# Gate and up projections of an FFN as seven products of quarters

## The chip, the cores and the metric

The kernel runs on one core of one Trainium2 chip. The metric is the device time of one execution in microseconds (us). Five engines work beside each other, each through its own instructions in order: PE (matmul; PEld is its weight load), DVE (vector), ACT (scalar), POOL (GpSimd) and SP (here it only issues DMAs). Matmuls read SBUF and write PSUM; DMAs move data between HBM and SBUF.

## The reference

Two layers of a decoder trunk on 512 tokens of width 1024. Each layer is a half-weight SwiGLU FFN, a token mixer (sparse attention and retention), cross-attention into 256 memory tokens, and a second half-weight FFN; each of them has an RMSNorm before and after it. All is float32. The FFN, which the change is about:

```python
def rms_norm(x, g):
    y = x * lax.rsqrt(jnp.mean(x * x, axis=-1, keepdims=True) + EPS)
    return y * g
def swiglu(x, w_gate, w_up, w_down):          # 1024 -> 2816 -> 1024
    return (jax.nn.silu(x @ w_gate) * (x @ w_up)) @ w_down
y = swiglu(rms_norm(x, ffn1_pre_g[l]), ffn1_w_gate[l], ffn1_w_up[l], ffn1_w_down[l])
x = x + 0.5 * rms_norm(y, ffn1_post_g[l])
```

## The kernel before, in words

Activations lie transposed: 8 tiles `x[c]` of 128 features by 512 tokens. A product of float32 precision is made of three matmuls on numbers split into a high and a low part (`mm3`, L113 to L116: high x high, high x low, low x high). The splits cost an ACT copy (the high part) and a DVE subtraction (the low part): for weights in `unit` (L85, L86), for activations in `split` (L122, L123) and `split_x` (L183, L184).

An FFN has 22 blocks of 128 hidden features, in three groups of 8, 7 and 7. For a block, `ffn` loads two weight units of 128 x 1024 (gate and up, 512 KB each, `nc.sync.dma_start`, three load buffers `raw`, four split buffers `whi` and `wlo`), and runs 2 x 8 chunks x 3 matmuls of 512 columns into two PSUM tiles `ps_gu`. L274 to L280 multiply by the inverse norm `bc`, form the SwiGLU with a tanh, and split the result into `hh` and `hl`. After a group comes its down projection: 8 output chunks `ps_dn`, each with 3 matmuls per block, added into `y[c]` (L299 copies in the first group, L301 adds later). In the last group the squares of `y[c]` are summed (`sumsq`, L153 on ACT and L154 on POOL, the last one on DVE), then `postnorm` takes the inverse norm through PE transposes and a Newton iteration on DVE, adds to `x[c]` and splits it for the next stage.

The last FFN of the program ends in `down_halves`: the last group of 7 blocks is done for the first 256 tokens, then for the others, and the norm and the output of the first half lie beside the matmuls of the second. `filler` and `prep` are pieces of cross-attention's keys, values and memory splits, put between stages.

The instructions are written per engine in the order that a scheduler of the framework draws up when the kernel is built: by program order, by what is ready, and by free buffers, with durations that it assumes. At run time every engine keeps that order. Load buffers are freed by the split's DVE part; the SP queue issues a load as soon as its buffer is free.

Of the kernel before, what the change touches and what calls it, by code (L numbers as in the profile page):

```python
# [9 lines left out]
F32 = mybir.dt.float32  # L10
# [7 lines left out]
P = 128  # L18
T = 512
# [6 lines left out]
GROUPS = ((0, 8), (8, 15), (15, 22))  # L26
# [21 lines left out]
def trunk(ctx: ExitStack, tc: tile.TileContext, a: dict, out: bass.AP):  # L48
# [9 lines left out]
    slots = {"b": 24, "xs": 16, "h": 16, "kv": 6}  # L58
# [20 lines left out]
    def unit(src, n):  # L79

        raw = wp.tile([P, 1024], F32, name="raw", tag="raw", bufs=3)[:, :n]
        nc.sync.dma_start(raw, src)
        hi = wp.tile([P, 1024], F32R, name="whi", tag="whi", bufs=4)[:, :n]
# [5 lines left out]
    def raw_unit(src, n):  # L89
        raw = wp.tile([P, 1024], F32, name="raw", tag="raw", bufs=3)[:, :n]  # L90
        nc.sync.dma_start(raw, src)
        return raw
# [4 lines left out]
    first = {0: unit(a["ffn1_gu"][0, 0, 0], 1024)}  # L97
    for c in range(1, 4):
        nc.sync.dma_start(x[c], a["xT"][c])
    first[1] = unit(a["ffn1_gu"][0, 0, 1], 1024)  # L100
# [12 lines left out]
    def mm3(ps, ah, al, bh, bl, start, stop):  # L113
        pe.matmul(ps, ah, bh, start=start, stop=False)  # L114
        pe.matmul(ps, ah, bl, start=False, stop=False)  # L115
        pe.matmul(ps, al, bh, start=False, stop=stop)  # L116
# [40 lines left out]
    def rms_cols(ssq, n, width):  # L157
# [6 lines left out]
        dve.tensor_reduce(t, ps[:, :width].rearrange("p (j n) -> p j n", n=P), axis=AX.X, op=ALU.add)  # L164
        v = tiny("rms_v", nt)
        dve.tensor_scalar(v, t, 1.0 / n, EPS, op0=ALU.mult, op1=ALU.add)
        return newton(v, nt)
# [17 lines left out]

    def gcols(l, col):
        return small[l][:, col : col + NC]

    def prenorm():

        xh, xl = [h for h, _ in xs], [lo for _, lo in xs]
        xs.clear()
        ssq, part = None, None
# [9 lines left out]
        return xh, xl, cols, bc  # L203

    def postnorm(y, ssq, gains, nxt, ts_=slice(0, T)):

        w = ts_.stop - ts_.start
        ps = row_bc(rms_cols(ssq[:, ts_], D, w), w // P)
        for c in range(NC):
# [3 lines left out]
            split_x(c, nxt, ts_)  # L213
# [43 lines left out]
    def ffn(l, which, gains, nxt, filler=None, prep=None, halves=False):  # L257
        gu, dn = FF_UNITS[which]
        if filler:
            filler()  # L260
        xh, xl, cols, bc = prenorm()
        y, ssq = [None] * NC, None
        for gi, (f0, f1) in enumerate(GROUPS):
            hh, hl = [], []
            for f in range(f0, f1):
                w = [first.pop(b) if b in first else unit(a[gu][l, f, b], 1024) for b in range(2)]
                pss = [acc("ps_gu") for _ in range(2)]
                for ts_ in HALVES if halves and f == 0 else (slice(0, T),):
                    for (wh, wl), ps in zip(w, pss):
                        for k in range(NC):  # L270
                            s = slice(k * P, (k + 1) * P)
                            mm3(ps[:, ts_], wh[:, s], wl[:, s], xh[k][:, ts_], xl[k][:, ts_], k == 0, k == NC - 1)
                g1 = big("g1")
                dve.tensor_tensor(g1, pss[0], bc, op=ALU.mult)  # L274
                th = big("th")
                act.activation(th, g1, AF.Tanh, scale=0.5)
                u1 = big("u1")
                dve.tensor_tensor(u1, pss[1], bc, op=ALU.mult)  # L278
                dve.scalar_tensor_tensor(g1, th, 1.0, g1, op0=ALU.add, op1=ALU.mult)
                dve.scalar_tensor_tensor(u1, g1, 0.5, u1, op0=ALU.mult, op1=ALU.mult)  # L280
                h_, l_ = split(u1, "h", tag="h")
                hh.append(h_)
                hl.append(l_)
            n = f1 - f0
            last = gi == len(GROUPS) - 1
            if prep and last:
                prep()
            if last and nxt is None:
                down_halves(a[dn][l], f0, n, hh, hl, y, gains)
                return  # L290
            for c in range(NC):
                wh, wl = unit(a[dn][l, c][:, f0 * P : f1 * P], n * P)
                ps = acc("ps_dn")
                for k in range(n):
                    s = slice(k * P, (k + 1) * P)
                    mm3(ps, wh[:, s], wl[:, s], hh[k], hl[k], k == 0, k == n - 1)
                if gi == 0:
# [4 lines left out]
                if last:  # L302
                    ssq = sumsq(ssq, y[c], c, dve if c == NC - 1 else pool)
        postnorm(y, ssq, gains, nxt)

    def down_halves(src, f0, n, hh, hl, y, gains):

        w = []
        for c in range(NC):
            if c < 4:  # L310
                wh, wl = unit(src[c][:, f0 * P : (f0 + n) * P], n * P)
                w.append([(wh[:, k * P : (k + 1) * P], wl[:, k * P : (k + 1) * P]) for k in range(n)])
            else:
                raw = raw_unit(src[c][:, f0 * P : (f0 + n) * P], n * P)
                parts = []
                for k0 in (0, 4):
                    m = min(4, n - k0) * P
                    h_, l_ = big("dh", F32R, tag="xs")[:, :m], big("dl", F32R, tag="xs")[:, :m]
# [624 lines left out]
```

## Time and profile before

| | |
|---|---|
| time of the kernel, median of 3 | 2508.59 us (2506.43 to 2508.6) |
| time of the profiled execution | 2508.29 us |
| its span, first to last instruction | 2506.5 us |
| busy: PE, PEld, DVE, ACT, POOL | 2431.5, 2020.5, 1400.2, 902.4, 258.8 us |
| mean granted TensorE clock | 0.995 |
| DMA | 233.62 MB, mean 93 GB/s |

Matmuls overlap in the pipeline, so the duration of one (389 ns) is longer than its distance from the next; what a matmul costs is read from the distance. Idle time of an engine is put down to the instruction that ended it. A line of the profile (L114) is a line of the kernel printed above, and can be that of a helper which many stages call.

### The profile page before, as it was taken

How to read it: one execution, taken by the hardware profiler on the slowest of the kernel's cores; microseconds unless marked ns; L12 is line 12 of the kernel's file. 1: busy time of each engine (PE TensorE's matmuls, PEld its weight loads, DVE VectorE, ACT ScalarE, POOL GpSimd, SP SyncE). 2: the span in 40 equal slices, each digit the busy share in tenths (PEclk: the TensorE clock that was granted, in tenths of full speed). 3: DMA queues.
4: the chain of work that ended last, by engine and by line, in shares of the span. 5: the costliest groups of instructions: out<-in, count | busy, mean ns of one | idle time of the engine just before them, and what ended most of it. 6: DMA issues, size and time to landing. Idle time of an engine off the chain costs nothing. (4 is left out here: it accounts for less than half of the span.)

```text
span 2506.5 us, 30782 instructions
## 1 busy us (share of the span) xinstructions
PE 2431.5 (97%) x12052; PEld 2020.5 (81%) x12052; DVE 1400.2 (56%) x2536; ACT 902.4 (36%) x1480; POOL 258.8 (10%) x218
## 2 busy tenths in 40 slices
PE   8999999999999999999999999999999998999997
PEld 6888878888877878888878888868888777888887
DVE  6434458465776484344484344584657766634454
ACT  4322243255344443222343222332553443322222
POOL 0000022001040120000120000130010402100002
PEclk9999999999999999999999999999999999999999
DMA  4333333411232233233333333324112222232321
GB/s 173 98 100 94 99 121 108 143 45 34 76 109 84 93 101 93 101 93 100 110 98 96 101 93 101 106 89 150 44 35 70 93 76 68 86 100 92 102 90 62
DMA packets 74593, 233.62 MB, mean 93 GB/s; under 512 B 8272, under 2 KB 17744, under 8 KB 74448
## 3 DMA queue, kind: packets, MB, share of 16 engines
q1 hardware_dynamic: 65232, 222.21, 27.9%
q10 hardware_dynamic: 9216, 9.44, 1.2%
q8 instruction: 95, 1.56, 0.3%
q14 instruction: 50, 0.41, 0.1%
HBM read 229.53 MB, written 2.10 MB: 92 GB/s over the span
## 5 line engine op out<-in xcount | busy, mean ns | idle before, releaser
L85 ACT ACTIVATE whi<-raw 128x1024 fp32r<-128x1024 f32 (+2 forms) x402 | 417.8, 1041 | 1097.6 <-PE ps_gu L115 324.0
L86 DVE TENSOR_TENSOR wlo<-raw,whi 128x1024 fp32r<-128x1024 f32 (+2 forms) x402 | 491.2, 1223 | 292.7 <-ACT whi L85 284.4
L114 PE MATMUL ps_gu<-xsh,whi 128*128 128x512 f32 (+1 forms) x1424 | 552.3, 389 | 13.8 <-ACT whi L85 9.3
L115 PE MATMUL ps_gu<-xsl,whi 128*128 128x512 f32 (+1 forms) x1424 | 555.0, 390 | 9.9 <-DVE xsl L184 9.7
L116 PE MATMUL ps_gu<-xsh,wlo 128*128 128x512 f32 (+1 forms) x1424 | 552.8, 388 | 0.0
L115 PEld LDWEIGHTS ps_gu<-xsl,whi 128*128 128x128 f32 x1424 | 268.6, 189 | 71.2 <-DVE xsl L184 17.7
L114 PEld LDWEIGHTS ps_gu<-xsh,whi 128*128 128x128 f32 x1424 | 269.0, 189 | 69.2 <-ACT whi L85 9.2
L116 PEld LDWEIGHTS ps_gu<-xsh,wlo 128*128 128x128 f32 x1424 | 268.8, 189 | 55.4 <-DVE wlo L86 1.8
L154 POOL TENSOR_TENSOR ssq<-ssq,sq 128x512 f32<-128x512 f32 (+1 forms) x84 | 131.4, 1564 | 1708.7 <-ACT sq L153 1705.6
L115 PE MATMUL ps_dn<-hl,whi 128*128 128x512 f32 (+1 forms) x704 | 268.5, 382 | 2.4 <-DVE hl L123 2.4
L114 PE MATMUL ps_dn<-hh,whi 128*128 128x512 f32 (+1 forms) x704 | 268.2, 381 | 0.0
L116 PE MATMUL ps_dn<-hh,wlo 128*128 128x512 f32 (+1 forms) x704 | 268.0, 381 | 0.0
L278 DVE TENSOR_TENSOR u<-ps_gu,rstd_bc 128x512 f32<-128x512 f32 x88 | 60.8, 691 | 215.4 <-PE ps_gu L116 215.3
L274 DVE TENSOR_TENSOR g<-ps_gu,rstd_bc 128x512 f32<-128x512 f32 x88 | 60.8, 691 | 183.9 <-PE ps_gu L116 179.4
L115 PEld LDWEIGHTS ps_dn<-hl,whi 128*128 128x128 f32 x704 | 132.3, 188 | 28.9 <-DVE hl L123 3.8
L114 PEld LDWEIGHTS ps_dn<-hh,whi 128*128 128x128 f32 x704 | 132.4, 188 | 26.2 <-ACT hh L122 0.5
L116 PEld LDWEIGHTS ps_dn<-hh,wlo 128*128 128x128 f32 x704 | 132.4, 188 | 25.1
L301 DVE TENSOR_TENSOR y<-ps_dn,y 128x512 f32<-128x512 f32 x56 | 38.7, 691 | 132.3 <-PE ps_dn L116 132.3
L115 PE MATMUL ps_fm<-xsl,whi 128*128 128x512 f32 x256 | 103.2, 404 | 4.0 <-DVE xsl L184 3.8
L114 PE MATMUL ps_fm<-xsh,whi 128*128 128x512 f32 x256 | 103.0, 404 | 0.0
L116 PE MATMUL ps_fm<-xsh,wlo 128*128 128x512 f32 x256 | 101.3, 396 | 0.6 <-DVE wlo L86 0.6
L612 ACT ACTIVATE p<-p,smx 128x512 f32<-128x512 f32 (+3 forms) x128 | 70.5, 552 | 87.2 <-DVE smx L610 87.0
(226 smaller groups left out, 3723.0 us busy)
## 6 DMA issues: line engine op xcount, KB each, us to landing
raw<-in_ffn_gu_dram SPq DMA_DIRECT2D x176, 512.0 KB, 3.3
raw<-in_ffn_dn_dram SPq DMA_DIRECT2D x64, 448.0 KB, 3.3
raw<-in_ffn_dn_dram SPq DMA_DIRECT2D x32, 512.0 KB, 3.5
raw<-in_win_fm_dram SPq DMA_DIRECT2D x32, 512.0 KB, 3.3
raw<-in_wk_dram SPq DMA_DIRECT2D x16, 512.0 KB, 3.5
raw<-in_cmp_w_dram SPq DMA_DIRECT2D x16, 512.0 KB, 3.7
raw<-in_wout_dram SPq DMA_DIRECT2D x16, 512.0 KB, 3.5
raw<-in_wv_dram SPq DMA_DIRECT2D x16, 512.0 KB, 3.5
```

Of the source, the lines that this page charges most:

```text
L85: act.activation(hi, raw, AF.Copy)
L86: dve.tensor_tensor(lo, raw, hi.bitcast(F32), op=ALU.subtract)
L114: pe.matmul(ps, ah, bh, start=start, stop=False)
L115: pe.matmul(ps, ah, bl, start=False, stop=False)
L116: pe.matmul(ps, al, bh, start=False, stop=stop)
L154: eng.tensor_tensor(acc_t, acc_t, sq, op=ALU.add)
L274: dve.tensor_tensor(g1, pss[0], bc, op=ALU.mult)
L278: dve.tensor_tensor(u1, pss[1], bc, op=ALU.mult)
L301: dve.tensor_tensor(y[c], ps, y[c], op=ALU.add)
L612: act.activation(pr[i], pr[i], AF.Exp, bias=m, scale=-1.0, accum_out=sums[:, i : i + 1])
```

## The change

Two blocks make a pair; an FFN has 11 pairs. The weights of gate and up for a pair lie in HBM as four quarters q0 to q3 of 128 x 1024 (first block with input chunks 0 to 3, the same with chunks 4 to 7, second block likewise; each with gate and up side by side). The operands are x in quarters as well: chunks 0 to 3 or 4 to 7, first or second half of the tokens.

The first two pairs of an FFN are computed as before from quarters (`plain`). The other nine use seven products instead of eight (the Winograd form of Strassen's scheme): seven weight operands (four quarters and sums of them) by seven operands of x (pieces and sums of them, made once per FFN in `combos`), each 2 x 4 x 3 matmuls of 256 columns. Sums of products are made partly in PSUM (a product added to what an earlier one left) and partly by DVE and POOL. The weight sums are made by DMAs of POOL's queue which add a quarter from HBM to a tile in SBUF (`accum_op`). Weight splits go from 4 to 7 per pair. The signs are folded into the operands, and the inverse norm before the up product is left out and put into the norm after the FFN (`cols` in `rms_cols`).

The down projection works on groups of 4 blocks, and of 2 in the end; the group of two pairs is projected after the products of the pair that follows. Load buffers go from 3 to 6, work slots (tag "b") from 24 to 18, "xs" from 16 to 24, "h" from 16 to 8; the mixer's queries and keys move into load buffers, and some tiles change their tag. The first pair's operands and weights, and the filler, are asked for ahead of the norm of the stage before (`ffn_first`).

```diff
-    slots = {"b": 24, "xs": 16, "h": 16, "kv": 6}
+    slots = {"b": 18, "xs": 24, "h": 8, "kv": 6, "onsa": 1}
...
+    def split_s(c, g, ts_=slice(0, T)):
+        k = c % 4
+        for u, half in enumerate(HALVES):
...
+            if c < 4:
+                if k % 2 == 0:
+                    ops["t", u] = big("x1h", F32R, tag="xs"), big("x1l", F32R, tag="xs")
+                ops[u + 1, k] = hi, lo = [t[:, HALVES[k % 2]] for t in ops["t", u]]
+                act.activation(hi, x[c][:, half], AF.Copy, scale=g[:, c : c + 1])
+                dve.scalar_tensor_tensor(lo, x[c][:, half], g[:, c : c + 1], hi.bitcast(F32), op0=ALU.mult, op1=ALU.subtract)
...
+    def combos(g):
...
+        for k in range(4):
+            b = []
+            for c in (k, k + 4):
+                xg = big("xg")
+                act.activation(xg, x[c], AF.Copy, scale=g[:, c : c + 1])
+                b += [xg[:, HALVES[0]], xg[:, HALVES[1]]]
+            t5, t7 = big("xt"), big("xt")
+            dve.tensor_tensor(t5[:, :256], b[1], b[0], op=ALU.subtract)
+            pool.tensor_tensor(t7[:, :256], b[3], b[1], op=ALU.subtract)
+            dve.tensor_tensor(t5[:, 256:], b[3], t5[:, :256], op=ALU.subtract)
+            pool.tensor_tensor(t7[:, 256:], t5[:, 256:], b[2], op=ALU.subtract)
...
+    class Pair:
...
+        def add(self, t, q):
+            pool.dma_start(t, self.quarter(q), accum_op=ALU.add)
+            return t
+        def raw(self, n):
+            if n == 1:
+                self.t = self.load(0)
+                return self.t
+            if n == 7:
+                return self.add(self.t, 2)
+            if n == 5:
+                self.u = self.load(2)
+                return self.add(self.u, 3)
+            if n == 6:
+                return self.add(self.u, 0)
+            if n == 3:
+                return self.add(self.u, 1)
+            return self.load({2: 1, 4: 3}[n])
...
+        def product(self, n, ps, o, start=True):
+            if n not in self.w:
+                self.weights(n)
+            wh, wl = self.w.pop(n)
+            for u in range(2):
+                for k in range(4):
+                    s = slice(u * 512 + k * P, u * 512 + (k + 1) * P)
+                    xh, xl = ops[o, k]
+                    mm3(ps[:, HALVES[u]], wh[:, s], wl[:, s], xh, xl, start and u == 0 and k == 0, u == 1 and k == 3, not start)
...
+        def p1(self):
+            self.A = acc("ps_gu")
+            self.product(1, self.A, 1)
+            self.s1 = self.kept(self.A)
+        def p2(self):
+            self.product(2, self.A, 3, start=False)
+        def p7(self):
+            self.C = aux("ps_gc")
+            self.product(7, self.C, 7)
+            self.s7 = self.kept(self.C)
+        def p5(self):
+            self.B = acc("ps_gu")
+            self.product(5, self.B, 5)
+            self.s5 = self.kept(self.B)
+        def p6(self):
+            self.product(6, self.B, 6, start=False)
+            self.e = big("ge")
+            dve.tensor_tensor(self.e, self.B, self.s1, op=ALU.subtract)
+            pool.tensor_tensor(self.s5, self.e, self.s5, op=ALU.subtract)
+        def p4(self):
+            self.product(4, self.C, 8, start=False)
+            dve.tensor_tensor(self.s7, self.e, self.s7, op=ALU.subtract)
+            dve.tensor_tensor(self.s5, self.s5, self.C, op=ALU.subtract)
+        def p3(self):
+            ps = acc("ps_gu")
+            self.product(3, ps, 4)
+            dve.tensor_tensor(self.e, ps, self.e, op=ALU.subtract)
+        def swiglu(self, bc, hs, tag="h"):
+            for q in ((self.A, self.e), (self.s5, self.s7)):
+                g1, th = big("g1"), big("th")
+                for ts_, t in zip(HALVES, q):
+                    dve.tensor_tensor(g1[:, ts_], t[:, :256], bc[:, ts_], op=ALU.mult)
+                act.activation(th, g1, AF.Tanh, scale=0.5)
+                dve.scalar_tensor_tensor(g1, th, 1.0, g1, op0=ALU.add, op1=ALU.mult)
+                for ts_, t in zip(HALVES, q):
+                    dve.tensor_tensor(g1[:, ts_], g1[:, ts_], t[:, 256:], op=ALU.mult)
+                hs.append(split(g1, "h", 0.5, tag=tag))
...
+        ORDER = "p1", "p5", "p2", "p7", "p6", "p4", "p3"
...
+        for p in pairs[:2]:
+            for f in range(2):
+                p.plain(f, bc, hs)
+                if p is pairs[0] and f == 1:
+                    combos(gcols(l, G_F1PRE if which == "ffn1" else G_F2PRE))
+        f0 = 0
+        for p in pairs[2:]:
+            final = p is pairs[-1]
+            for n in ORDER:
+                getattr(p, n)()
+            if len(hs) == 4:
+                down(f0, hs, False)
+                f0, hs = f0 + 4, []
+            p.swiglu(bc, hs, "xs" if final else "h")
...
+        down(f0, hs, True)
+        postnorm(y, state["ssq"], gains, nxt, cols=(cols, sq))
```

## Rows read from the trace of the kernel before

**Rows 1.** The page, parts 1 and 2: busy time and share; granted clock by fortieths.

```profile
PE 2431.5 (97%) x12052; PEld 2020.5 (81%) x12052; DVE 1400.2 (56%) x2536; ACT 902.4 (36%) x1480; POOL 258.8 (10%) x218
PEclk9999999999999999999999999999999999999999
```

**Rows 2.** Windows: us, busy (x instructions) of each engine, PEclk, DMA share, GB/s.

```profile
145.00:221.00 76.00, 76.00 (x337) 62.90 (x337) 37.27 (x46) 22.59 (x28) 0.00 (x0) 1.00 0.30 92
221.00:259.00 38.00, 38.00 (x169) 31.47 (x168) 15.96 (x18) 8.60 (x9) 0.00 (x0) 1.00 0.33 103
755.00:839.00 84.00, 83.96 (x414) 66.44 (x413) 57.72 (x115) 43.69 (x88) 0.00 (x0) 0.99 0.28 88
2108.00:2152.00 44.00, 35.30 (x209) 30.43 (x208) 35.93 (x90) 19.06 (x34) 15.69 (x17) 0.92 0.19 61
```

**Rows 3.** Timeline of PE: start, us, instruction; a run of 48 matmuls of 512 columns.

```profile
864.70 0.39 PE L114 MATMUL ps_o<-xoh,whi 128*128 128x512 f32 x1
...
875.35 0.39 PE L116 MATMUL ps_o<-xoh,wlo 128*128 128x512 f32 x1
875.58 0.28 PE L114 MATMUL ps_mk<-memg,whi 128*128 128x256 f32 x1
```

**Rows 4.** Timeline of PE in the last down projection: matmuls of 256 columns, 21 apart.

```profile
2489.35 0.28 PE L114 MATMUL ps_dn<-hh,dh 128*128 128x256 f32 x1
...
2491.87 0.28 PE L114 MATMUL ps_dn<-hh,dh 128*128 128x256 f32 x1
```

**Rows 5.** Groups by form, DVE and ACT: xcount | busy us, mean ns | idle before.

```profile
L86 DVE TENSOR_TENSOR wlo<-raw,whi 128x1024 fp32r<-128x1024 f32 x336 | 420.0, 1251 | 276.1 <-ACT whi L85 273.7 <-PE ps_o L116 1.8
L274 DVE TENSOR_TENSOR g<-ps_gu,rstd_bc 128x512 f32<-128x512 f32 x88 | 60.8, 691 | 183.9 <-PE ps_gu L116 179.4 <-ACT rstd_bc L202 4.4
L301 DVE TENSOR_TENSOR y<-ps_dn,y 128x512 f32<-128x512 f32 x56 | 38.7, 691 | 132.3 <-PE ps_dn L116 132.3
L329 DVE TENSOR_TENSOR y<-ps_dn,y 128x256 f32<-128x256 f32 x16 | 6.7, 422 | 18.9 <-PE ps_dn L116 18.7
L85 ACT ACTIVATE whi<-raw 128x1024 fp32r<-128x1024 f32 x336 | 355.6, 1060 | 909.5 <-issue 301.8 <-PE ps_gu L115 235.1 <-PE ps_dn L115 168.8
L122 ACT ACTIVATE hh<-u 128x512 fp32r<-128x512 f32 x88 | 55.7, 633 | 63.2 <-DVE u L280 63.1
```

**Rows 6.** Groups by form, POOL; the largest two.

```profile
L154 POOL TENSOR_TENSOR ssq<-ssq,sq 128x512 f32<-128x512 f32 x65 | 116.6, 1794 | 1054.2 <-ACT sq L153 1051.5 <-issue 1.2
L154 POOL TENSOR_TENSOR ssq<-ssq,sq 128x256 f32<-128x256 f32 x19 | 14.8, 777 | 654.4 <-ACT sq L153 654.1
```

**Rows 7.** The page, parts 3 and 6: the main DMA queue; issues with landing time.

```profile
q1 hardware_dynamic: 65232, 222.21, 27.9%
...
raw<-in_ffn_gu_dram SPq DMA_DIRECT2D x176, 512.0 KB, 3.3
```

**Rows 8.** Waits of the SP queue: us in total, times, longest.

```profile
SPq L82 <- DVE wlo L86: 2035.9, 361, 37.4
```

**Rows 9.** Timeline of DVE, 899 to 907 us; POOL adds until 904.15.

```profile
899.34 1.98 DVE L86 TENSOR_TENSOR wlo<-raw,whi 128x1024 fp32r<-128x1024 f32 x1
...
905.89 1.21 DVE L86 TENSOR_TENSOR wlo<-raw,whi 128x1024 fp32r<-128x1024 f32 x1
```

**Rows 10.** Timeline of POOL over the same stretch.

```profile
898.49 5.66 POOL L154 TENSOR_TENSOR ssq<-ssq,sq 128x512 f32<-128x512 f32 x3
```

**Rows 11.** Timeline of DVE in the tail: halves' evictions, norm and last adds.

```profile
2471.25 0.42 DVE L329 TENSOR_TENSOR y<-ps_dn,y 128x256 f32<-128x256 f32 x1 [2.10 <-PE ps_dn L116]
...
2481.20 0.74 DVE L329 TENSOR_TENSOR y<-ps_dn,y 128x256 f32<-128x256 f32 x2
...
2493.40 0.43 DVE L154 TENSOR_TENSOR ssq<-ssq,sq 128x256 f32<-128x256 f32 x1 [0.55 <-ACT sq L153]
```

**Rows 12.** Timeline of all engines at the end of the second FFN.

```profile
1253.71 1.74 POOL L154 TENSOR_TENSOR ssq<-ssq,sq 128x512 f32<-128x512 f32 x1 [3.02 <-ACT sq L153]
...
1258.98 0.68 DVE L154 TENSOR_TENSOR ssq<-ssq,sq 128x512 f32<-128x512 f32 x1
```

More of the change, by code (lines that the diff above doesn't have):

```diff
@@ L111, in trunk, with mm3 @@
             lst.append(hg)
[L113 to L116, printed above, removed]
+    def mm3(ps, ah, al, bh, bl, start, stop, more=False):
+        pe.matmul(ps, ah, bh, start=start, stop=False, skip_group_check=more)
+        pe.matmul(ps, ah, bl, start=False, stop=False, skip_group_check=more)
+        pe.matmul(ps, al, bh, start=False, stop=stop, skip_group_check=more)
     def split(src, name, gain=None, tag="b"):
@@ L202, in prenorm, with postnorm @@
         act.activation(bc, ps, AF.Copy)
-        return xh, xl, cols, bc
-    def postnorm(y, ssq, gains, nxt, ts_=slice(0, T)):
+        return cols, bc
+    def postnorm(y, ssq, gains, nxt, ts_=slice(0, T), cols=None):
         w = ts_.stop - ts_.start
-        ps = row_bc(rms_cols(ssq[:, ts_], D, w), w // P)
+        if ts_.start == 0 and nxt[0]:
+            nxt[0]()
+        ps = row_bc(rms_cols(ssq[:, ts_], D, w, cols), w // P)
         for c in range(NC):
@@ L212, in postnorm @@
             (dve if c == 0 else pool).tensor_tensor(x[c][:, ts_], x[c][:, ts_], t, op=ALU.add)
-            split_x(c, nxt, ts_)
+            (split_s if nxt[0] else split_x)(c, nxt[1], ts_)
     def out_proj(src, l, oh, ol):
@@ L286, in ffn, with ffn_first, run @@
[L286 to L292, printed above, removed]
+                for ts_, t in zip(HALVES, q):
+                    dve.tensor_tensor(g1[:, ts_], g1[:, ts_], t[:, 256:], op=ALU.mult)
+                hs.append(split(g1, "h", 0.5, tag=tag))
+    warm = {}
+    def ffn_first(l, which, filler=None):
+        def run():
+            if filler:
+                filler()
+            ps_ = warm[l, which] = [Pair(a[FF_UNITS[which][0]][l], j) for j in range(NPAIR)]
+            for q in range(2):
+                ps_[0].w["q", q] = split_unit(ps_[0].load(q))
+        return run
@@ new lines, in ffn, with weights, down @@
+    def ffn(l, which, gains, nxt, prep=None):
+        dn = FF_UNITS[which][1]
+        pairs = warm.pop((l, which))
+        y, state = [None] * NC, {"ssq": None}
+        ORDER = "p1", "p5", "p2", "p7", "p6", "p4", "p3"
+        def weights(f0, n):
+            per = 1024 // (n * P)
+            for c0 in range(0, NC, per):
+                raw = wp.tile([P, 1024], F32, name="raw", tag="raw", bufs=6)
+                nc.sync.dma_start(raw.rearrange("p (c n) -> p c n", c=per),
+                                  a[dn][l, c0 : c0 + per, :, f0 * P : (f0 + n) * P].rearrange("c p n -> p c n"))
+                wh, wl = split_unit(raw)
+                for u in range(per):
+                    yield c0 + u, [(wh[:, s], wl[:, s]) for s in
+                                   (slice((u * n + k) * P, (u * n + k + 1) * P) for k in range(n))]
+        def down(f0, hs, final):
+            n = len(hs)
+            for c, w in weights(f0, n):
@@ L301, in ffn @@
                     dve.tensor_tensor(y[c], ps, y[c], op=ALU.add)
[L302 to L318, printed above, removed]
-                    act.activation(h_, raw[:, k0 * P : k0 * P + m], AF.Copy)
-                    dve.tensor_tensor(l_, raw[:, k0 * P : k0 * P + m], h_.bitcast(F32), op=ALU.subtract)
-                    parts += [(h_[:, k * P : (k + 1) * P], l_[:, k * P : (k + 1) * P]) for k in range(m // P)]
-                w.append(parts)
-        for ts_ in HALVES:
+                if final:
+                    state["ssq"] = sumsq(state["ssq"], y[c], c, dve if c == NC - 1 else pool)
@@ L687, in to_fm @@
                 pe.transpose(pt[:, i * P : (i + 1) * P], tiles[i], ident)
-            h_, l_ = split(pt, "o", sm[:, G_NSA + c : G_NSA + c + 1], tag="h")
+            h_, l_ = split(pt, "o", sm[:, G_NSA + c : G_NSA + c + 1], tag="xs" if c < 4 else "h")
             oh.append(h_)
@@ L818, in xattn @@
                     mm3(ps, v_h[:, fs], v_l[:, fs], pTh[m], pTl[m], m == 0, m == 1)
-                h_, l_ = split(ps, "xo", tag="h")
+                h_, l_ = split(ps, "xo", tag="xs" if f < 4 else "h")
                 oh.append(h_)
```

170 lines of the change are left out of this document (108 added, 62 removed).

## The prediction

> **What bounds the kernel now.** I read the page's first two parts, then windows over stages, then a timeline of single matmuls. PE is busy 97% of the span, at full granted clock (2.4 GHz) in all forty slices [rows 1]. Inside an FFN there is nothing else: in 76 us of gate and up projections PE is busy for all 76 us, DVE for 37, ACT for 23; in the 38 us of down projection after it PE again fills the stretch [rows 2]. So a microsecond less of matmuls there is a microsecond less of time, as long as DVE, ACT and the DMAs can follow. Where PE is not full is the border between stages: in the 44 us at the entry of the last FFN it is busy 35 [rows 2].
>
> The price of a matmul is its distance from the next. With 512 columns 48 of them take 875.58 - 864.70 = 10.88 us, 226.7 ns each [rows 3]. With 256 columns 21 take 2491.87 - 2489.35 = 2.52 us, 120.0 ns each [rows 4]. Two halves thus cost 240.0 where a whole costs 226.7: each matmul has 13.3 ns that don't shrink with its columns.
>
> **The change, part by part.** The sum is made against the profiled execution, 2508.3 us (span 2506.5 and 1.8 around it), 0.3 under the median of 2508.59.
>
> *Seven products.* A pair of blocks had 2 blocks x 2 (gate, up) x 8 chunks x 3 = 96 matmuls of 512 columns: 21.76 us. It gets 7 products x 2 x 4 x 3 = 168 of 256 columns: 20.16 us. The arithmetic falls by 1/8, but the 13.3 ns come 72 times more often, so the gain is 1.60 us a pair, and 57.6 us for 9 pairs x 4 FFNs. The Trainium skill (TensorE: Matmul & The Clock Gate, Back-to-back issue gap) gives columns / 2.4 + 2.5 ns for a warm matmul. By that, an estimate, the pair would go from 20.7 to 18.3 us, the 36 pairs would give 85 us, and the time would come out at 2460 us. This trace disagrees at both widths (226.7 and 120.0 ns for 215.8 and 109.2), so it gets no chance of its own.
>
> *Plain pairs.* The other 2 pairs read quarters: per block 48 matmuls of 256 and 24 of 512, 5.76 + 5.44 = 11.20 us against 48 of 512, 10.88. For 16 blocks +5.1, less 0.6 for the one that already ran in halves: +4.5 us.
>
> *Down projection.* 22 blocks x 8 x 3 matmuls stay, in groups of 4,4,4,4,4,2 for 8,7,7. On PE that is free. In the last FFN only 2 blocks instead of 7 are done in token halves, which takes cover away from the tail. Now the first half's last eviction is at 2471.25, DVE then does that half's norm until 2481.20, PE goes on with 20.16 us of second-half matmuls meanwhile, and the last square sum is at 2493.40, 13.1 us before the end [rows 11]. After, the second half has 5.76 us of matmuls, done before DVE comes back; its evictions (8 x 0.42 [rows 5]) and POOL's chain of square sums (6 x 0.78 [rows 6]) follow in a row, so that I put the last square sum some 16 us behind the first half's end instead of 22.2. Counted with PE: before 20.16 + 35.3 to the end, after 27.2 (five blocks whole) + 5.8 + 29.1 = 62.1 us, so +7 us.
>
> *End of the other three FFNs.* With 2 blocks in the last group PE makes an output chunk in 6 x 0.2267 = 1.36 us, but its square sum takes POOL 1.79 [rows 6]. Six of those are a chain of 10.7 us that starts about 4 us into the 10.9 us group, and with the last add ends some 4.5 us behind PE. Now a chunk has 21 x 0.2267 = 4.76 us, the sums come 5.27 us apart, POOL is done long before the last one [rows 12], and that is one eviction, one square and one add behind PE: 0.69 + 0.63 + 0.68 = 2.0 us. +2.5 us each, +7; at nothing where memory keys or values fill PE meanwhile.
>
> *Entry.* Operands come in half-token pieces, with gate and up of the first block together. Three entries stay paced by the same chain; I take 0, from -5 to +5 each. The last loses something: chunks 4 to 7 of the first block need both token halves. +4 us, of 0 to 8; PE is idle 8.7 of the 44 us there already [rows 2].
>
> *Buffers elsewhere.* The work slots go from 24 to 18; the mixer gives six back by moving queries and keys to the load buffers. Cross-attention doesn't, and PE is full there now [rows 2], so a stall is seen: +3 us over both layers, of 0 to 10.
>
> *DVE and ACT in a product pair.* DVE: 7 weight splits x 1.25, 4 differences x 0.69, and for two blocks 2 x (4 half products x 0.42 + 2 x 0.69) [rows 5]: 8.75 + 2.76 + 6.12 = 17.6 us. The down projection adds per pair 2 splits and 4 evictions, 5.3 us: 22.9 of PE's 20.16 + 10.88 = 31.0 us. ACT: 9 splits x 1.06 and some 7 passes x 0.63 = 14 us. Both fit on average. Down projection comes behind every second pair only, so in the pair without it DVE has 17.6 of 20.2 us. I take 0.3 us of stall a pair, +11 us; the ends are 0 and, were DVE's 17.6 to grow by a third, 23.5 for 20.2 in 16 such pairs, +53.
>
> *Weight sums by DMA.* No accumulating DMA is in this trace, nor any issued by POOL. Nearest is a plain load of the same 512 KB: 3.3 us to landing [rows 7]. The queue moved 222.21 MB in 27.9% of 2506.5 us [rows 7], 318 GB/s while busy, so 1.65 us of the 3.3 are transfer. An accumulation can't land sooner than the load it contains (lower end 3.3); it must also read what it adds to, 5.0 with one more transfer; 10 is three loads one behind the other (upper end). I take 6 us with POOL's issue. What it may cost follows from the order 1,5,2,7,6,4,3: one tile carries q2 (+q3) for product 5, +q0 for 6, +q1 for 3, each addition waiting for the split before it. With four split buffers, the split of 5 can start when the product four places ahead of it ends, 5.8 us before product 1; product 3 starts 17.3 us after product 1's start. Those 23 us hold two additions and three splits of 1.06 + 1.25: an addition may take 8.0 us. At 6 it hides. DMA time per pair: 6 loads x 1.65 and 4 additions x 3.3 = 23 of 31 us, so that hides too, less comfortably. Behind a late addition stand on POOL only the next additions and one subtraction a pair; on ACT and DVE the splits behind it, and then PE.
>
> POOL also slows DVE: a split took 1.98 us while POOL was adding, and 1.21 just after [rows 9, 10]. DVE lost 0.77 of 1.98 us, 39%; one subtraction of about 1.8 us a pair costs it 0.7. The Trainium skill (SBUF — State Buffer, Who interferes with whom) says that a DVE instruction with two SBUF inputs contends with a GpSimd instruction that reads SBUF, and infers that making a DMA's descriptors isn't such a read. The first half agrees with the rows (1.98 for 1.21 us). By the second half, an estimate, the four additions would cost DVE nothing, and rival 2 below would fall back to the forecast; no run here shows it.
>
> *Loads.* SP's queue waits mostly for a load buffer to be freed (2036 us behind the split [rows 8]); six buffers for three let it run ahead, and the extra loads find their place.
>
> Sum: -57.6 + 4.5 + 7 + 7 + 4 + 3 + 11 = -21.1; 2508.3 - 21.1 = 2487 us.
>
> **The rivals.**
> *1. The additions land late (slower).* From 8.0 us on, product 3 waits in each pair that follows another without down projection between: 4 per FFN, 16 in all, 2 us for each microsecond, until at 10.6 the other pairs follow too. At 10 us: 16 x 2 x 2.0 = 64, and 2487 + 64 = 2551 us. It turns into a loss at 8.7 us (16 x 2 x 0.66 = 21). For it: the landing is unknown, and three dependent additions a tile; the 16 DMA engines would be three quarters busy, where the load's 3.3 was measured at a third. Against: both cheaper bounds hide.
> *2. DVE is the bound between down projections.* If the issue of an addition takes POOL the part of a load's landing that isn't transfer, 1.65 us, and slows DVE as its adds do, a pair loses 4 x 1.65 x 39% = 2.6 us more: 17.6 + 0.7 + 2.6 = 20.9 against 20.2. With another 0.4 us of waiting that is 1.1 us in 16 pairs: 2487 + 18 = 2505 us, no change. For it: DVE 1400 us now [rows 1], and some 9 us more in each pair. Against: the down projection, where DVE is busy 16 of 38 us [rows 2], lets it catch up.
> *3. Everything hides.* Pair stalls and the small losses at borders are nothing, only the tail stays: 2508.3 - 57.6 + 4.5 + 7 = 2462 us. For it: PE has not one gap in an FFN today, with only three load buffers. Against: no cover is left in the pairs without down projection.
> That the change doesn't do what it says would be seen in the matmul count; the code gives no sign of it.
>
> **How the numbers follow.** Forecast (faster, 2468 to 2500) 0.48; rival 3 (2454 to 2468) 0.17; rival 2 (2500 to 2514) 0.12; rival 1 (2514 and above) 0.23. 0.2%, about 5 us, is what a measurement of this kernel can tell from no change. Faster: 0.48 + 0.17 + 0.02 of rival 2 = 0.67; same 0.08; slower: 0.23 and 0.02 of rival 2 = 0.25. The range goes from 2456 to 2552: it leaves out the best of rival 3 and additions of over 10 us.
>
> **What would show it.** Gate and up matmuls of 256 columns 120 ns apart, and 20.2 us a product pair between waits: the first step. PE waiting for a split in front of product 3 or 6, with ACT waiting for the addition's landing over 8 us: rival 1. DVE without idle time in the pairs without down projection and PE waiting for low parts: rival 2. The last eviction of the first token half some 29 us before the end: the tail. The prediction is wrong if 256 columns cost over 126 ns (then 36 x 168 x 6 ns = 36 us of the gain is gone), or if the additions land past 8.7 us.

## The result, and the profile after

The changed kernel takes 2543.25 us (2542.61 to 2546.03, 4 runs), the kernel before beside it 2507.51 (2505.92 to 2508.6): a ratio of 1.0145, 95% interval 1.0128 to 1.0163. It is 36 us slower, where 21 us less were forecast.

The page of the changed kernel: busy time of each engine, the queue of the additions (packets, MB, share of 16 engines), and what an addition takes from issue to landing. Lines such as L341 are from here on lines of the changed kernel.

```profile
PE 2402.8 (95%) x14860; PEld 2132.7 (84%) x14860; DVE 1696.1 (67%) x3018; ACT 1101.6 (43%) x1760; POOL 461.6 (18%) x430
q0 software_dynamic: 20736, 75.51, 17.7%
raw<-in_ffn_gu_dram POOLq DMA_DIRECT2D x144, 512.0 KB, 5.7
```

PE is busy 28.7 us less than before [rows 1], and yet the span is 34.3 us longer: 63 us of idle time have come in. The next two tables show where. Windows by stage, of the kernel before and then of the changed one, in this order: first FFN, mixer, cross-attention, second FFN, and the same for the second layer (us; busy of PE, PEld, DVE, ACT, POOL; PEclk, DMA share, GB/s).

```profile
0.00:377.10 377.10, 364.95 (x1597) 299.58 (x1597) 185.44 (x247) 124.62 (x165) 20.68 (x21) 1.00 0.36 115
377.10:722.10 345.00, 335.97 (x1998) 288.90 (x1997) 215.40 (x559) 143.13 (x301) 48.26 (x49) 1.00 0.27 84
722.10:875.60 153.50, 147.20 (x698) 117.04 (x697) 101.47 (x170) 71.71 (x127) 28.77 (x16) 0.99 0.29 93
875.60:1256.70 381.10, 375.88 (x1697) 309.71 (x1696) 196.40 (x258) 121.84 (x157) 26.63 (x16) 1.00 0.31 100
1256.70:1638.80 382.10, 375.69 (x1697) 309.71 (x1696) 196.88 (x258) 122.01 (x157) 26.16 (x16) 1.00 0.32 100
1638.80:1975.00 336.20, 327.46 (x1877) 275.38 (x1877) 210.37 (x549) 140.88 (x299) 49.58 (x48) 1.00 0.25 80
1975.00:2108.60 133.60, 128.28 (x634) 101.80 (x633) 90.84 (x158) 61.40 (x111) 27.46 (x15) 1.00 0.24 75
2108.60:2506.50 397.90, 376.05 (x1864) 318.36 (x1864) 203.35 (x338) 116.84 (x165) 31.31 (x37) 0.98 0.27 86
```

```profile
0.00:374.30 374.30, 353.90 (x2340) 326.22 (x2341) 261.00 (x367) 173.84 (x238) 71.38 (x73) 1.00 0.66 171
374.30:729.70 355.40, 342.13 (x1998) 292.40 (x1997) 214.97 (x561) 143.17 (x301) 51.76 (x50) 0.97 0.25 81
729.70:880.70 151.00, 145.43 (x698) 116.18 (x697) 101.04 (x170) 71.42 (x127) 28.27 (x16) 1.00 0.28 94
880.70:1266.10 385.40, 368.40 (x2441) 340.73 (x2440) 270.75 (x378) 172.48 (x229) 71.64 (x67) 0.98 0.60 148
1266.10:1648.80 382.70, 366.47 (x2441) 339.17 (x2441) 270.46 (x380) 172.23 (x230) 75.26 (x70) 0.98 0.60 148
1648.80:2000.30 351.50, 336.70 (x1877) 281.51 (x1876) 210.06 (x551) 141.53 (x300) 53.22 (x51) 0.97 0.24 78
2000.30:2134.10 133.80, 128.26 (x634) 101.83 (x632) 90.85 (x158) 61.28 (x111) 27.45 (x15) 1.00 0.23 75
2134.10:2540.80 406.70, 361.55 (x2440) 334.63 (x2440) 276.95 (x454) 165.60 (x229) 82.68 (x90) 0.95 0.52 127
```

Three things stand in these tables. The four FFNs together are 11 us longer, though their matmuls are 55 us less (recorded matmuls by width, times the distances of [rows 3, 4]). The mixers, whose matmuls are the same in number, are 10.4 and 15.3 us longer. And the clock, 0.98 to 1.00 in all eight stages before, is 0.95 to 0.98 in five: of the 55 us that PE should be less busy 26 are missing, and matmuls at the lower level are busy longer.

Inside an FFN the stall stands in the pairs. Two product pairs in a row should take 2 x 20.16 = 40.3 us; the 16 stretches of two pairs, from the first gate matmul to the down projection, together take 34.7 us more. This sum is called the pair stalls below. In the stretch shown here all of it (3.9 us) falls into the second pair. First the window of the whole stretch, then the chain of waits into the second pair (start us, us, what):

```profile
1125.90:1170.10 44.20, 41.98 (x337) 41.78 (x336) 28.55 (x35) 19.71 (x24) 7.12 (x7) 0.96 0.65 152
```

```profile
1141.98 1.44 DVE gk L425
...
1144.10 1.22 DVE wlo L89
1145.33 0.29 issue
1145.62 5.86 DMA raw<-in_ffn_gu_dram
1151.58 0.33 ACT whi L88
1151.92 0.63 issue
1152.55 0.61 ACT hh L132
1153.16 0.52 ACT th L439
1153.68 0.49 ACT gk L375
1154.21 0.58 PE ps_gu L121
```

The addition (of q0, for product 6) is issued when the split before it has read the tile, and lands 5.86 us later. ACT's next split (`whi`) has stood at the head of its queue for that landing; behind it in the same queue stand two instructions of the SwiGLU and the kept copy `gk` of product 1, which had ended at 1149.0. Product 2 is added to the PSUM tile that this copy reads, so it needs the copy, and it starts at 1154.21. In the window from there to 1156.00 the granted clock is 0.50, and its matmuls are 0.21 us apart instead of 0.12. The same seen by line: what the additions (L341) took and who waited for them (us, times), PE's largest wait in the pairs, and that window.

```profile
L341 POOL DMA_DIRECT2D raw<-in_ffn_gu_dram x144: 862/865/1197, 29.7 to 2466.5; - x144
...
  ACT whi L88: 185.5, 61
...
DMA to landing us min/median/max: 5.2/5.7/8.6
```

```profile
PE ps_gu L121 <- ACT gk L375: 24.9, 16, 2.3
1154.20:1156.00 1.80, 1.78 (x8) 1.79 (x9) 1.76 (x5) 1.46 (x3) 0.86 (x1) 0.50 0.29 38
```

The lower clock is the lesser part. It comes in three of the 16 stretches, behind waits of 2.13, 2.22 and 2.01 us; they take 4.4, 3.9 and 3.7 us too much. In the other 13 the stall is hardly more than one wait of 1.1 to 2.3 us. Behind the wait of 2.27 us before product 2 in the first of them the clock stayed up:

```profile
127.50:132.00 4.50, 4.31 (x36) 4.31 (x37) 3.58 (x6) 2.21 (x4) 0.86 (x1) 1.00 0.62 99
```

### The profile page after: what moved, and what is told of

Same layout as the page of the kernel before. It is cut to its first block, busy times and chain, and to the rows that moved or that the text cites. A ratio compares the mean times of both kernels' runs of the same rounds, so it can differ in the third digit from the quotient of the medians.

```text
span 2540.8 us, 37896 instructions
## 1 busy us (share of the span) xinstructions
PE 2402.8 (95%) x14860; PEld 2132.7 (84%) x14860; DVE 1696.1 (67%) x3018; ACT 1101.6 (43%) x1760; POOL 461.6 (18%) x430
## 3 DMA queue, kind: packets, MB, share of 16 engines
q0 software_dynamic: 20736, 75.51, 17.7%
## 4 chain that ended last, share of the span: by engine, by line
PE 43%; DVE 5%; issue 2%; DMA 2%; ACT 2%; POOL 1%; POOLq 0%; ACTq 0%; DVEq 0%
PE ps_gu L121 4%; PE ps_gu L122 4%; PE ps_gu L123 4%; PE ps_dn L121 3%; PE ps_dn L122 3%; PE ps_dn L123 3%; DMA raw<-in_ffn_gu_dram 2%; PE ps_po L829 1%; PE ps_gc L121 1%; PE ps_gc L123 1%; PE ps_gc L122 1%; PE ps_o L121 1%; PE ps_o L122 1%; PE ps_o L123 1%; PE ps_fm L123 1%
## 5 line engine op out<-in xcount | busy, mean ns | idle before, releaser
L89 DVE TENSOR_TENSOR wlo<-raw,whi 128x1024 fp32r<-128x1024 f32 (+1 forms) x506 | 619.7, 1231 | 410.6 <-ACT whi L88 408.2
L88 ACT ACTIVATE whi<-raw 128x1024 fp32r<-128x1024 f32 (+1 forms) x506 | 529.5, 1054 | 797.3 <-DMA raw<-in_ffn_gu_dram 185.5
L341 POOL DMA_DIRECT2D raw<-in_ffn_gu_dram x144 | 125.7, 891 | 974.9 <-DVE wlo L89 730.4
L121 PE MATMUL ps_gu<-x3h,whi 128*128 128x256 f32 (+1 forms) x704 | 216.7, 308 | 24.9 <-ACT gk L375 24.9
L122 PE MATMUL ps_gu<-x3l,whi 128*128 128x256 f32 (+1 forms) x704 | 215.6, 306 | 1.2 <-DVE x3l L218 1.2
L123 PE MATMUL ps_gu<-x3h,wlo 128*128 128x256 f32 (+1 forms) x704 | 215.0, 305 | 0.0
L121 PE MATMUL ps_gc<-x7h,whi 128*128 128x256 f32 x576 | 163.3, 283 | 0.9 <-ACT gk L375 0.9
L121 PE MATMUL ps_gu<-x5h,whi 128*128 128x256 f32 x576 | 163.0, 283 | 0.0
L122 PE MATMUL ps_gu<-x5l,whi 128*128 128x256 f32 x576 | 163.0, 283 | 0.0
L123 PE MATMUL ps_gc<-x7h,wlo 128*128 128x256 f32 x576 | 163.0, 283 | 0.0
L122 PE MATMUL ps_gc<-x7l,whi 128*128 128x256 f32 x576 | 163.0, 283 | 0.0
```

The lines of the kernel that those rows point to most:

```text
L121: pe.matmul(ps, ah, bh, start=start, stop=False, skip_group_check=more)
L122: pe.matmul(ps, ah, bl, start=False, stop=False, skip_group_check=more)
L123: pe.matmul(ps, al, bh, start=False, stop=stop, skip_group_check=more)
L341: pool.dma_start(t, self.quarter(q), accum_op=ALU.add)
```

## The experiments

All are edits of the changed kernel (2543 us) unless said otherwise. The kernel before had a median of 2507 to 2509 us beside each; ratios are against it, with the 95% interval in brackets. The changed kernel's own interval is 1.0128 to 1.0163. Of the single edits e2, e4, e13 and e14 lie clear below it; those of e3, e6 and e17 overlap it, so their 4 to 6 us are uncertain, and e5, e7 and e8 can't be told from it.

**Where the loss is.** First all pairs by plain quarters, then three places that the stage table points to.

```diff
-            for n in ORDER:              # e1_plain: all eleven pairs plain
-                getattr(p, n)()
...
+            for f in range(2):
+                p.plain(f, bc, mine, "xs" if len(hs) == 4 else "h")
...
-        q = pair_tile("q") + pair_tile("q")      # e2_mixer
+        q = [big("q", tag="xs") for _ in range(4)]
...
-        ksel = pair_tile("ksel")
+        ksel = [big("ksel", tag="xs") for _ in range(2)]
...
+        ps = row_bc(rms_cols(ssq[:, ts_], D, w, cols), w // P)   # e3_norm_first: moved up
         if ts_.start == 0 and nxt[0]:
             nxt[0]()
-        ps = row_bc(rms_cols(ssq[:, ts_], D, w, cols), w // P)
...
-            pool.tensor_tensor(self.s5, self.e, self.s5, op=ALU.subtract)   # e4_dve
+            dve.tensor_tensor(self.s5, self.e, self.s5, op=ALU.subtract)
```

> All eleven pairs are computed plainly from quarters (no products, no combos, no accumulating DMAs); slots, load buffers, groups of four and the borders stay as in the changed kernel. Theory A (the products pay about what was worked out, and the time is lost at the borders: mixers +26 us, FFN entries +23, tail and group ends +18, and about 30 in waits of the product pairs): 36 pairs cost 22.4 for 20.2 us of PE, +81, and the pair waits of some 30 us go, so 2543 + 50 = 2590 us. Theory B (the product pairs themselves cost more than they save, by DVE, ACT and the additions): 2500 to 2530 us.

> The mixer's queries and selected keys go into slots of the tag xs, which are free until the retention part, and no longer into three of the six load buffers; all else is the changed kernel. Theory A (the mixers lose 26 us because these tiles take load buffers from the weights at the mixer's start, so that fewer weight units are split before the norm, and PE runs dry in the compress part): the mixers come back to 338 and 345 us, 2543 - 20 = about 2523 us. Theory B (it is the work slots, 18 for 24, or the later arrival of x): no change, within 3 us of 2543.

> In postnorm the inverse norm (transposes, Newton, broadcast) is written ahead of the next FFN's filler and first weights instead of behind them. Theory A (the memory-key products stand on PE ahead of the norm's transposes, and nothing is left to fill the 8 to 10 us of the norm's chain; both FFN entries with a filler lose 7 us): 2543 - 13 = about 2530 us. Theory B (the entries lose by the half-token pieces and the doubled splits): within 3 us of 2543.

> The subtraction that product 6 gives to POOL runs on DVE instead. Theory A (POOL's add blocks a DVE instruction with two SBUF operands for as long as it runs, so it costs DVE 1.5 us and saves it 0.7, and DVE is what delays the copies that product 2 waits for): pair waits fall from about 30 to 15 us, 2543 - 10 to -15 = about 2530 us. Theory B (DVE has room, and the additions' landing sets the waits): 2543 to 2550 us.

e1_plain: 2586.92 us, 1.0314 [1.03, 1.0328]. Against plain quarters the seven products do pay, 44 us; the rest of the change costs more. Plain quarters are themselves dearer than the pairs of the kernel before (22.40 for 21.76 us by [rows 3, 4], 23 us over 36 pairs), so against those the products gain some 21 us. The forecast's 57.6 less the 34.7 of pair stalls gives nearly the same, 23. e2_mixer: 2527.64, 1.0077 [1.0063, 1.0091], 16 us less. The mixers' windows in it:

```profile
374.80:725.00 350.20, 339.12 (x1997) 290.39 (x1996) 214.93 (x561) 143.59 (x300) 49.71 (x50) 0.98 0.26 82
1642.70:1981.60 338.90, 328.59 (x1878) 274.94 (x1877) 210.00 (x551) 141.45 (x301) 52.90 (x50) 1.00 0.25 79
```

355.4 became 350.2 and 351.5 became 338.9: 18 of the 26 us lost in these windows came from queries and keys lying in buffers that the next weights are loaded into. e3_norm_first: 2538.91, 1.0121 [1.0107, 1.0134], only 4 us: at two entries the first gate matmul stands 12.9 and 15.7 us behind the first filler matmul instead of 19.6 and 22.0, and by the first product pair 4.5 and 3.9 us of that are left. The whole kernel gains half of that; its pair stalls are 36.9 us in this trace, though nothing in the pairs was changed. e4_dve: 2529.39, 1.009 [1.0076, 1.0103], 14 us as expected. The subtraction beside POOL's (L425), by form in the changed kernel and then in e4_dve:

```profile
L425 DVE TENSOR_TENSOR gk<-ge,gk 128x512 f32<-128x512 f32 x36 | 52.0, 1444 | 0.5
```

```profile
L425 DVE TENSOR_TENSOR gk<-ge,gk 128x512 f32<-128x512 f32 x36 | 24.7, 685 | 0.0
```

DVE gets back 759 ns of 1444 in each pair and no longer waits for POOL's result; the pair stalls fall from 34.7 to 18.8 us. (Kernels whose pairs and additions are untouched, e2, e3, e5, e7 and e8, have 33.1 to 40.4 us in their traces; a difference within these bounds says nothing.)

**Order and clock.** Four further places, and sums of the edits.

```diff
+                if n == "p1" and pend:      # e6_swiglu_later: behind the next pair's p1
+                    pend.swiglu(bc, hs)
...
-            if len(hs) == 4:               # e5_tail: last FFN, 6 blocks (not 2) in token halves
+            if len(hs) == 4 and not (final and nxt is None):
...
+                # e7_entry_halves: first block of the last FFN, halves outermost
+                for i, half in enumerate(HALVES if q == 0 and by_half else ()):
+                    for k in range(4):
...
+    def keep(n):                           # e8_keep_pe: keep(30) at two entries,
+        ps = aux("ps_idle")                # twice, behind the norm's transposes
+        for _ in range(n):
+            pe.matmul(ps[:, :256], idle[:, :P], idle, start=True, stop=True)
```

> Left as it is: everything but the order. The swiglu of a pair that has no down projection behind it is written one product later, behind the first product of the next pair, so that ScalarE's kept copy of that product's PSUM tile stands ahead of it and not behind it. Theory (TensorE's 1.5 to 2.5 us wait in front of product 2 is the kept copy queued behind the swiglu, 16 pairs): the row of ps_gu waiting for gk falls from 24.9 us to a few, and the time to about 2518 us. Rival (VectorE is simply the bound in those pairs, the wait moves to the low parts of a later product): the waits sum up the same and the time stays within 5 us of 2543.

> In the last FFN alone the last down projection takes 6 blocks in token halves instead of 2, so that the second half's 17.3 us of matmuls stand beside the norm of the first half. Theory (of the 18.2 us that TensorE stands still after the last half's matmuls began 10 to 12 are cover lost by the shorter last group): 2533 us. Rival (what is lost there is VectorE's and GpSimd's own chain, and the extra splits of weights take the place of the wait): within 4 us of 2543.

> In the last FFN the first block's gate and up products over input chunks 0 to 3 run for the first token half entirely and then for the second, where the changed kernel alternates the halves after every three matmuls. Theory (the 6.1 us wait of TensorE for the eviction y and the half-level clock at 2144 to 2158 us come from TensorE's order, which needs the second half's norm after three matmuls): the last entry shortens by 5 to 8 us, time 2537 us. Rival (the entry is paced by VectorE's chain for the second half, whatever TensorE does first): within 3 us of 2543.

> At two FFN entries 2 x 30 matmuls of 256 columns, whose result nobody reads, are put into the two idle times of TensorE (behind the norm's first and second transposes, 4.4 and 4.5 us each; 30 x 0.12 = 3.6 us). Nothing else is changed. Theory (part of the loss at the borders is the clock, which falls to half behind these idle times for some 10 us: 6.6 to 7.3 us of matmuls at half rate per entry): the granted clock stays at 1.00 there and the time falls by 2 x 3.4 = 7 us, to 2536 us. Rival (the slow matmuls there are late operands and not the clock, or the clock falls all the same): no gain, 2543 to 2548 us.

e6_swiglu_later: 2537.51, 1.0119 [1.0106, 1.0133]; 6 us and not 25. PE's waits for kept copies in it show why: product 2's fell, another product took them over.

```profile
PE ps_gc L121 <- ACT gk L375: 13.4, 17, 1.1
...
PE ps_gu L121 <- ACT gk L375: 6.3, 14, 1.1
```

e5_tail: 2541.04, 1.0131 [1.0114, 1.0147]: not to be told from the changed kernel by its interval, though the stretch from the last down projection to the end is 5 us shorter in its trace (55.0 for 59.8); its pair stalls are 37.5 us there. e7_entry_halves: 2542.56, 1.0137 [1.0122, 1.0152]: nothing, as the rival had it. PE's order is not what paces that entry; that VectorE's norm of the second half does fits, but was not tried by itself. e8_keep_pe: 2550.04, 1.0157 [1.0136, 1.0178]: no gain. 16 us from just behind the norm's first transposes at one of the entries, in the changed kernel and then in e8_keep_pe:

```profile
1278.00:1294.00 16.00, 7.28 (x34) 6.61 (x33) 13.29 (x32) 4.21 (x9) 5.38 (x5) 0.57 0.40 100
```

```profile
1284.80:1300.80 16.00, 13.33 (x104) 12.34 (x102) 14.80 (x30) 4.52 (x10) 6.37 (x5) 1.00 0.39 100
```

The clock stayed at 1.00 there, and the time did not fall: from the first filler matmul to the first product pair the two entries take 74.7 and 75.0 us, for 73.1 and 73.3 in the changed kernel. My theory that the clock costs time at these entries is refuted. DVE is busy 13.3 of the 16 us, and PE waits for its operands, fast or slow. The entries make 3 of the 7 us by which e8 is longer; its pair stalls are 40.4 us in this trace.

> The three edits of the first experiments together: queries and keys of the mixer in other buffers than the loads', the norm's transposes ahead of the products that fill, and the subtraction of GpSimd on VectorE. If their places are apart, as the theory has it, the gains add up: 16 + 4 + 14 = 34 us below the changed kernel, 2509 us, the time of the kernel before. If they take away the same slack (one engine's queue behind all of them), the sum is not above 20 us: 2523 us.

> All five edits together. If every loss is a wait at a place of its own: 2543 - 34 - 10 (tail) - 10 (what the subtraction on VectorE leaves of the wait for the kept copy, 13.7 us) = 2489 us, faster than the kernel before. If the last two don't pay: 2505 to 2512 us.

> The five edits together (2498 us) and the order of e7_entry_halves in the last entry. If that entry is a loss of its own: 2492 us. If it is paced by VectorE: 2498 us.

e9_all3 (e2, e3 and e4): 2505.38, 0.999 [0.9982, 0.9999]. 38 us below the changed kernel where 34 had been added up, so the three losses lie at places of their own. e10_all5 (and e5, e6): 2497.93, 0.9968 [0.9955, 0.998], not the 2489 hoped for. e11_best (and e7): 2497.41, 0.9954 [0.9941, 0.9968]; e7 adds nothing here either.

**The additions.** The pair stalls of e10 and e11 (18 us) had no owner yet. So the adding itself was taken away. The same DMAs copy their quarter over the tile, so the weight sums are left out and the results are other numbers; every instruction and the order of PE, DVE, ACT and POOL are the same.

```diff
-            pool.dma_start(t, self.quarter(q), accum_op=ALU.add)
+            pool.dma_start(t, self.quarter(q))
```

> The four DMAs of a pair on GpSimd's queue copy their quarter over the tile instead of adding it to the tile; the same DMAs at the same places, so the weights are other numbers (the sums are left out) and every engine's instructions and order stay as they are. Theory (the additions land in 5.7 us, inside the 8.0 us that the order leaves them, and hide): the landing falls toward the 4.1 us of a plain load and the time stays within 4 us of 2543. Rival (the additions come late, or their reading of the tile takes SBUF from VectorE): 15 us or more below.

2511.35 us, 1.0014 [1.0005, 1.0023]: 32 us less. My theory fell, the rival was right. The same stretch of two pairs as above, the queue, the landing, POOL's issue and ACT's wait for the landings in e13_no_add:

```profile
1112.59:1153.05 40.46, 40.46 (x338) 40.36 (x336) 28.13 (x35) 20.18 (x24) 5.67 (x7) 1.00 0.56 171
```

```profile
q0 software_dynamic: 20736, 75.51, 9.5%
```

```profile
raw<-in_ffn_gu_dram POOLq DMA_DIRECT2D x144, 512.0 KB, 4.0
```

```profile
L341 POOL DMA_DIRECT2D raw<-in_ffn_gu_dram x144: 527/528/697, 29.7 to 2435.1; - x144
...
  ACT whi L88: 66.0, 36
```

PE is busy for all of 40.46 us; the pair stalls of the whole kernel are 2.3 us instead of 34.7, and ACT waits 66.0 us for these landings instead of 185.5. An addition costs 1.7 us more to landing than a copy, 0.34 us more of POOL's time, and nearly twice the share of the queue's engines; these three together decide. Whether by its rate or by its place in a chain of waits, the last five runs asked.

```diff
-                return self.add(self.t, 2)           # e14_own_tile; e15: the same in e11
+                return self.add(self.load(0), 2)
...
-            self.s1 = self.kept(self.A)              # e17_keep_dve; e18: the same in e15
+            self.s1 = big("gk")
+            dve.tensor_copy(self.s1, self.A)
...
-        hi = wp.tile([P, 1024], F32R, name="whi", tag="whi", bufs=4)[:, :n]   # e16, in e11
+        hi = wp.tile([P, 1024], F32R, name="whi", tag="whi", bufs=5)[:, :n]
...
-        raw = wp.tile([P, 1024], F32, name="raw", tag="raw", bufs=6)[:, :n]
+        raw = wp.tile([P, 1024], F32, name="raw", tag="raw", bufs=5)[:, :n]
```

> The weights of product 7 (q0 + q2) are made in a tile of their own: q0 is loaded a second time, and the addition to it no longer waits until the split of product 1 has read the first tile. Everything else stays; 36 x 4 loads of 512 KB become 36 x 5. Theory (the stall of a pair is this addition's place in the chain: ScalarE's split stands at the landing, and the kept copy of product 1 behind it): the row of ps_gu waiting for gk goes from 24.9 us to under 8, the pair stalls of 34.7 us to about 12, time 2520 us. Rival (the additions' transfer is the limit, so more loads make it worse): 2543 us or more.

> e11_best (2497 us) with the tile of its own for product 7. Its pair stalls are 17.7 us in the profile. Theory: they fall to some 8, time 2488 us. Rival (more loads): 2497 us or more.

> e11_best with five split buffers for weights instead of four, paid by one load buffer less (5) and two work slots less (16). Each split, and each addition behind it, can start one product (2.9 us) earlier; the DMAs are the same. Theory (chain of waits): pair stalls of 17.7 us fall below 5, time 2484 us. Rival (the rate of the additions, or the load buffer that is missing): 2497 us or more.

> The kept copy of product 1's PSUM tile (36 of 512 columns, 0.58 us each) is made by VectorE and not by ScalarE; nothing else changes. Theory (product 2 waits for this copy, which stands in ScalarE's queue behind a split that waits for an addition): the wait of ps_gu for gk goes, pair stalls of 34.7 us fall to 15 or less, time 2525 us. Rival (VectorE stands behind the same split for its low part, or lacks the time): the wait only changes its name, 2540 us or more.

> e15_best_own (2493 us) with the kept copy of product 1 on VectorE. Theory: pair stalls of 15.1 us fall to some 6, 2485 us. Rival: 2493 us or more.

e14_own_tile: 2532.3, 1.0096 [1.0082, 1.011]: 11 us less with 18.9 MB more to load. So it is not the rate at which the loads can come, and this addition's place in the chain is part of the cost, but half of what was expected (pair stalls 22.7). e15_best_own: 2493.4, 0.9938 [0.9924, 0.9951], by its interval not to be told from e11. e16_best_split5: 2503.54, 0.9984 [0.9975, 0.9992], a miss: starting splits earlier, with one load buffer and two work slots less, made the pair stalls 26.0 us; it changes more than one thing, and which of them did it was not tried. e17_keep_dve: 2538.6, 1.0124 [1.0109, 1.014]: 5 us less at most, the rival. The wait kept its place and changed its name, since DVE's queue stands behind the low part of the same split (the order drawn up for PE changed with this edit too):

```profile
PE ps_gu L121 <- DVE gk L403: 22.0, 16, 1.9
```

e18_best_keep_dve: 2491.69, 0.9937 [0.9925, 0.995], not to be told from e15. These two beat the kernel before by 15 to 16 us.

## Why the prediction was wrong

The step that failed first is "I take 0.3 us of stall a pair, +11 us", and with it "an addition may take 8.0 us. At 6 it hides". 34.7 us of pair stalls were measured for 11, and e13_no_add, which takes only the adding away, gives 32 of them back. The addition was priced right (6 us; 5.7 measured), and for the product that uses the sum it does hide. In the stretch above it is product 6 that uses it: the low part of its split ends at 1153.90, and the product starts at 1161.48.

```profile
1152.67 1.23 DVE L89 TENSOR_TENSOR wlo<-raw,whi 128x1024 fp32r<-128x1024 f32 x1 [1.13 <-ACT whi L88]
```

```profile
1161.48 0.28 PE L121 MATMUL ps_gu<-x5h,whi 128*128 128x256 f32 x1
```

What the sum left out is who else stands in the queue of the engine that waits. The prediction's list is "on ACT and DVE the splits behind it, and then PE"; the kept copies are not in it. ACT takes its instructions in order; its splits waited for the additions' landings 185.5 us in all, and the kept copies that the next product needs stood behind them. The stall came in front of product 2, which uses no sum at all. So rival 1 had the mechanism (late additions) with the wrong condition: they are late at 5.7 us, not from 8.0. That 2543 us lies within its bounds is luck; by its own price it gets there with a landing of 9.75 us (16 x 2 x 1.75 = 56). Neither of the two signs that the prediction names for being wrong came: the matmuls are 0.12 us apart, and the additions land before 8.7 us. What of the 32 us is the landing, what the longer issue on POOL and what the busier queue was not separated.

Second, "the mixer gives six back" was put at nothing, and "Buffers elsewhere" at +3. The mixers lost 25.7 us, cross-attention gained 2.3. e2_mixer returns 18 of them: buffers for loads are not free to lend in a stage that loads ahead. What the remaining 8 us are was not tried.

Third, "Three entries ... I take 0": from the first filler matmul to the first gate matmul the entries of the second and third FFN take 19.6 and 22.0 us for 12.9 and 13.0 before. An entry's cost is counted here to the first product pair (before: to the end of the fourth block), less the matmuls in it: 7.6 and 7.0 us more, the first FFN's 1.9 less, together 12.8. PE runs the filler first and then stands still twice for the norm; e3_norm_first changes that order and gets 4.5 and 3.9 us back there, 4 in the whole kernel.

Right were these. The seven products: 256 columns are 0.12 us apart and a pair without a wait takes 20.2 us, as e13's window shows. By their counts the matmuls are 54.7 us less; 1.6 of it is what the tail saves with fewer blocks in token halves, and the other 53.1 is the forecast (57.6 less 4.5). The last entry: +6.1 us for +4. The tail: 59.8 us from the last down projection for 55.8, and with one block (5.4 us) less in it 9.4 lost for 7; the first half's last eviction, at 2508.7, stands 32 us before the end where 29 were forecast:

```profile
2481.00:2540.80 59.80, 35.68 (x202) 30.47 (x200) 35.91 (x96) 11.95 (x23) 15.43 (x20) 0.82 0.10 36
```

The end of the other three FFNs was too dear: +0.6 us for +7. Sum of what was measured: -53.1 + 34.7 + 23.4 + 12.8 + 9.4 + 6.1 + 0.6 = +33.9 of 34.3 us in the span (23.4 are the mixers less cross-attention); 0.4 have no place.

Rival 2 was half right: DVE is slowed, but by POOL's subtraction and not by the issue of additions. That is the first link of the chain shown above: L425 there took 2.20 us beside the subtraction, and the split behind it, product 5's, ended at 1145.31. The prediction's sum lets it end 2.31 us after product 6 of the pair before, at 1142.6; so the addition came 2.7 us later than the sum has it. e4_dve, which takes the subtraction off POOL, lowers the pair stalls by 16 us. An addition's issue on POOL and DVE's split beside it, in the changed kernel (start us, us):

```profile
1145.62 0.89 POOL L341 DMA_DIRECT2D raw<-in_ffn_gu_dram  x1 [2.00 <-DVE wlo L89]
```

```profile
1145.83 1.21 DVE L89 TENSOR_TENSOR wlo<-raw,whi 128x1024 fp32r<-128x1024 f32 x1
```

The split took 1.21 us, as one with POOL idle [rows 9]. Here the Trainium skill (SBUF — State Buffer, Who interferes with whom) is borne out twice: a DVE instruction with two inputs in SBUF contends with GpSimd's reads of SBUF (1444 for 685 ns), and, as it infers, making a DMA's descriptors does not hold such an instruction up (1.21 us beside the issue seen here). By it rival 2 should have rested on the subtraction alone, as the forecast did with 0.7 us a pair; 0.76 were measured.

## What to carry to other kernels

A transfer that "hides" hides only if nothing else stands behind the instruction that waits for it: list what is queued on that engine, and price the wait for the whole queue. Where a tile is added to step by step, each step is a round of split, issue and landing; a second load of the start into a tile of its own can be cheaper than a place in that chain. Memory taken from a stage that is not being changed has to be priced there.

## What the runs showed of the hardware

An accumulating DMA of 512 KB into SBUF landed in 5.7 us where a copy at the same place took 4.0, kept the queue's engines busy 17.7% for 9.5% of the span with the same 75.51 MB, and held POOL 865 ns for 528. In three of 16 stretches of two pairs the granted clock fell to its lower level (1.2 GHz) behind a single wait of 2.0 to 2.2 us between matmuls that kept PE fully busy, and product 2 took some 1.5 us more for it; in another stretch it stayed at 1.00 behind a wait of 2.27 us. At the entry of the third FFN it fell with the first of two waits of 4.6 and 4.2 us, and keeping it up there was worth nothing.
